# A convolution's banks, copies and order inside a two-block transformer kernel

## The chip, the cores and the metric

The kernel runs on one core of a Trainium2 chip. The metric is the device time of one execution in microseconds. TensorE multiplies matrices into PSUM banks, VectorE and ScalarE work on tiles of 128 partitions, GpSimd does some of the sums, and SyncE issues most of the DMAs; ScalarE and GpSimd can issue DMAs too. Every engine works through its own queue in order and waits on semaphores for the others.

## The reference, cut to what matters

The whole computes two small models one after the other on 512 tokens of width 1024. The change touches the first layer only:

```python
h = rms_norm(x, even_norm_g[j])
z = h @ even_w_in[j] + even_b_in[j]
za = gelu(z[..., :2 * A_WIDTH]); zb = z[..., 2 * A_WIDTH:]
ya = chunked_spatial_gating(za, ...)   # u * (w_s @ layer_norm(v) + b_s), u and v halves of za
yb = conformer_conv(zb, ...)           # silu(layer_norm(causal_dwconv(a * sigmoid(g), 31 taps)))
x = x + concatenate([ya, yb], -1) @ even_w_out[j]
```

Behind it come a feed-forward block, a layer of attention, a second feed-forward block, and two layers of the second model.

## The kernel before

Activations lie transposed: eight tiles of 128 features by 512 tokens. A product is taken in three fp32r matmuls (`mm3`, line 671): the high part of the weight with the high and the low part of the activation, and the low part of the weight with the high part. Weights stream in blocks through three staging buffers `stg`; ScalarE rounds a block to its high part `whi`, VectorE makes the low part `wlo`, and with that the staging buffer is free for the next load, which SyncE issues (`load`, `w_split`, `w_next`).

The program is written by a planner. Its `Clock` (line 318) holds a time for each engine and one for all DMAs together; `Engine` (line 373) charges each operation as it is traced, a DMA by its bytes at 180 GB/s. Work beside the dense products is written as generators, which `spawn` puts in a list with the time at which their last operation ended. `pump` runs every generator that is due by TensorE's planned time, and goes on until nothing moves; `need` pumps until a flag is set. The planner thus fixes an order in which the operations are traced. A scheduler then orders each engine's queue by its own estimate, except where `ORDERED` (line 677) names the weight segment: there the engines given by letters (V VectorE, A ScalarE, T TensorE) keep the traced order, in a region that `part()` opens at the head of a dense product.

The first layer, `even()`, runs in this order: the rms norm of the eight input tiles (`rms_part`; the squares are summed in `sqacc`, and `rms_rstd` takes statistics with eight TensorE instructions, a reciprocal on VectorE, and eight more to spread the result), then the dense products "zb" (64 weight steps of three matmuls, four steps to a block; five output tiles side by side, then three), "v0" (eight weight steps, each for four token tiles: 96 matmuls, over four banks at once), "u0" (96 matmuls) and "eout" (two halves of 96). The first matmul needs only the first input tile.

Of "zb" come the four gated tiles `hp[j]` (`zb_done`). The convolution of tile 0 is 31 operations on VectorE (`conv`). Tiles 1 to 3 are convolved on TensorE (`conv_pe`): 16 copies of 32 partitions shift `hp[j]` into four pages `R`, then 32 calls (64 instructions) of 32-column matmuls accumulate in one bank, and ScalarE takes it out. `conv_out` norms the four tiles: the centre, an approximate mean from two of them, is subtracted from all, then the moments are summed, and the SiLU ends it. `v_done` and `u_done` make the gating: VectorE norms the values, TensorE multiplies them with `ws` (16 instructions for each of four tiles), and the product with GELU(u) is the input of "eout".

The eight PSUM banks are in rings: three "D" for dense products, two "S" (scores of the attention later, and the gating products here), one each of "P", "O" and "G". "zb" takes its banks from "DS", "v0" from "DP", the convolution from "O", the norm's centre and spread from "P" and "O".

## Time and profile before

| | us |
|---|---|
| median of three timed runs (2489.49 to 2492.5) | 2492.15 |
| the profiled execution | 2487.64 |
| its span | 2485.9 |
| TensorE busy in the span | 2412.0 |
| VectorE / ScalarE / GpSimd busy | 1404.0 / 1078.8 / 346.6 |

A busy TensorE is not TensorE at its peak, since the ends of matmuls are modelled; how many matmuls a stretch holds, and at what granted clock, tells more. Idle time of an engine that nobody waits for costs nothing. Nearly all instructions are recorded by one helper, line 402, so that groups are told apart by their tiles.

### The profile page before, as it was taken

To read this page: it belongs to the slowest core of one execution; us is meant where nothing else is said; L and a number is where in the kernel's file an instruction comes from. 1 tells how busy PE (TensorE), PEld (TensorE's weight loads), DVE (VectorE), ACT (ScalarE), POOL (GpSimd) and SP (SyncE) were. 2 spreads that over 40 slices of the span, in tenths; PEclk is the share of its full clock that TensorE was granted. 3 is DMA by queue.
4 is the path that set the end of the run, shared out by engine and by line. 5 is a ranking of instruction groups with operands and counts; after the bars stand their busy time and mean duration, and the time that the engine had idled before them with its cause. 6 is when DMAs were issued, how large, how long until landed. Compare 5 with 4: busy or idle time off the path is not lost.

```text
span 2485.9 us, 31565 instructions
## 1 busy us (share of the span) xinstructions
PE 2412.0 (97%) x12311; PEld 1957.1 (79%) x12311; DVE 1404.0 (56%) x2477; ACT 1078.8 (43%) x1740; POOL 346.6 (14%) x447
## 2 busy tenths in 40 slices
PE   9999999999999999999999999999999989999997
PEld 7578888888766788888786688888897767888887
DVE  6666746743874773673665474343577455634345
ACT  4345424433874442443655543232346454423133
POOL 2011000010432100003221340000231023100003
PEclk9999999999999999999999999999999999999998
DMA  5322323222112222223131123323222101222321
GB/s 176 121 68 93 102 94 100 95 95 84 60 61 72 91 97 94 101 94 107 59 98 47 50 62 100 102 94 100 87 71 77 44 26 52 95 100 94 102 94 60
DMA packets 64646, 212.33 MB, mean 85 GB/s; under 512 B 8208, under 2 KB 10672, under 8 KB 64496
## 3 DMA queue, kind: packets, MB, share of 16 engines
q1 hardware_dynamic: 61200, 202.03, 24.8%
q0 software_dynamic: 2576, 6.82, 0.9%
q8 instruction: 97, 1.59, 0.3%
q10 hardware_dynamic: 720, 1.46, 0.2%
q14 instruction: 53, 0.43, 0.1%
HBM read 205.03 MB, written 2.10 MB: 83 GB/s over the span
## 4 chain that ended last, share of the span: by engine, by line
PE 57%; DVE 5%; ACT 2%; issue 1%; POOL 1%; ACTq 0%; DVEq 0%; POOLq 0%
PE bank L402 57%; DVE pt L402 3%; ACT pt L402 1%; DVE x L402 1%; DVE wlo L402 1%; ACT L402 1%; POOL x L402 1%; ACT whi L402 0%; POOL pt L402 0%; DVE pl L402 0%; ACT x L402 0%; POOL sqacc L402 0%; DVE stat L402 0%; ACT kend L402 0%; ACTq L2012 0%
## 5 line engine op out<-in xcount | busy, mean ns | idle before, releaser
L402 PE MATMUL bank<-pt,whi 128*128 128x512 f32 (+1 forms) x6012 | 1789.6, 380 | 20.2 <-ACT pt L402 9.3
L402 PEld LDWEIGHTS bank<-pt,whi 128*128 128x128 f32 x6012 | 1099.5, 189 | 232.5 <-ACT pt L402 13.5
L402 PE MATMUL bank<-pt,wlo 128*128 128x512 f32 (+1 forms) x3006 | 1131.9, 377 | 1.6 <-DVE wlo L402 1.6
L402 DVE TENSOR_TENSOR wlo<-stg,whi 128x1024 fp32r<-128x1024 f32 (+2 forms) x387 | 471.8, 1221 | 467.6 <-ACT whi L402 461.2
L402 ACT CAST whi<-stg 128x1024 fp32r<-128x1024 f32 (+2 forms) x387 | 394.1, 1020 | 676.9 <-PE bank L402 596.4
L402 PEld LDWEIGHTS bank<-pt,wlo 128*128 128x128 f32 x3006 | 568.3, 189 | 106.4 <-DVE wlo L402 2.9
L402 ACT CAST pt<-pt 128x512 fp32r<-128x512 f32 (+1 forms) x226 | 139.4, 620 | 243.5 <-DVE pt L402 208.2
L402 DVE TENSOR_TENSOR pt<-pt,pt 128x512 fp32r<-128x512 f32 (+2 forms) x235 | 165.1, 706 | 84.1 <-ACT pt L402 81.1
L402 DVE TENSOR_TENSOR x<-x,bank 128x256 f32<-128x256 f32 (+1 forms) x294 | 135.4, 497 | 132.9 <-PE bank L402 126.6
L402 PE MATMUL bank<-pt,pt 128*64 128x128 f32 (+17 forms) x1192 | 185.3, 387 | 13.2 <-ACT pt L402 6.6
L402 POOL TENSOR_TENSOR pt<-pt,pt 128x256 f32<-128x256 f32 (+1 forms) x90 | 98.1, 1098 | 458.6 <-ACT pt L402 234.9
L402 PEld LDWEIGHTS bank<-pt,pt 128*64 128x64 f32 (+4 forms) x1192 | 101.6, 152 | 76.1 <-issue 44.3
L402 DVE SCALAR_TENSOR_TENSOR pt<-up,cst,pt 128x512 f32<-128x512 f32 x176 | 131.9, 749 | 6.5 <-ACT pt L402 3.4
L402 POOL TENSOR_SCALAR pt<-pt,stat 128x512 f32<-128x512 f32 (+3 forms) x160 | 99.7, 643 | 236.4 <-DVE stat L402 211.0
L402 ACT COPY pt<-bank 128x512 f32<-128x512 f32 (+4 forms) x157 | 79.8, 508 | 116.9 <-PE bank L402 115.5
L402 PE MATMUL bank<-whi,pt 128*128 128x512 f32 (+2 forms) x448 | 124.1, 353 | 2.7 <-DVE pt L402 2.2
L402 PEld LDWEIGHTS bank<-misc,pt 128*128 128x128 f32 (+1 forms) x632 | 78.8, 160 | 50.7 <-issue 25.6
L402 PE MATMUL bank<-misc,pt 128*128 128x128 f32 (+2 forms) x632 | 103.0, 273 | 9.6 <-ACT pt L402 4.4
L402 DVE TENSOR_TENSOR up<-bank,rstd 128x512 f32<-128x512 f32 x88 | 60.6, 688 | 87.9 <-PE bank L402 83.5
L402 DVE CUSTOM_DVE_ANT_0 pt<-bank,mask 128x512 f32<-128x512 f32 (+3 forms) x160 | 75.7, 486 | 56.9 <-PE bank L402 56.2
L402 POOL TENSOR_TENSOR x<-x,pt 128x256 f32<-128x256 f32 x24 | 22.2, 961 | 591.0 <-ACT pt L402 591.0
L402 ACT ACTIVATE pt<-pt,stat 128x256 f32<-128x256 f32 (+3 forms) x160 | 89.3, 559 | 32.8 <-DVE stat L402 31.6
(147 smaller groups left out, 1379.4 us busy)
## 6 DMA issues: line engine op xcount, KB each, us to landing
stg<-in_w_up_dram SPq DMA_DIRECT2D x88, 512.0 KB, 3.2
stg<-in_w_mu_dram SPq DMA_DIRECT2D x64, 512.0 KB, 3.4
stg<-in_w_md_dram SPq DMA_DIRECT2D x44, 512.0 KB, 3.4
stg<-in_w_dn_dram SPq DMA_DIRECT2D x33, 512.0 KB, 3.2
stg<-in_w_qk_dram SPq DMA_DIRECT2D x16, 512.0 KB, 3.2
stg<-in_w_tb_dram SPq DMA_DIRECT2D x16, 512.0 KB, 3.5
stg<-in_w_zb_dram SPq DMA_DIRECT2D x16, 256.0 KB, 3.3
stg<-in_w_eout_dram SPq DMA_DIRECT2D x8, 512.0 KB, 3.3
```

The source lines that it names most:

```text
L402: r = fn(*a, **k)
```

## The change

Five edits in the first layer and in the planner. The planner's DMA charge takes the number of partitions from the tile instead of 128, and is at least 0.5 us. "zb" is added to the segments in traced order, for VectorE and TensorE; "v0", until now in traced order on TensorE, is so on VectorE too. Of the sixteen copies of a convolution tile, those for groups 0 and 2 are issued by SyncE and those for 1 and 3 by ScalarE. The convolution takes a bank from "O" or, where that is in use, from "S". The centre comes from tiles 1 and 0, and tiles 2 and 3 follow.

```diff
@@ Engine.__getattr__
-                nbytes = 4 * 128 * (out.free_size() if callable(out.free_size) else out.free_size)
-                self.clock.op("DMA", nbytes / 180e3, [out], [src])
+                nbytes = 4 * (out.free_size() if callable(out.free_size) else out.free_size)
+                nbytes *= out.partition_size() if callable(out.partition_size) else out.partition_size
+                self.clock.op("DMA", max(nbytes / 180e3, 0.5), [out], [src])
@@ tile_kernel
-    ORDERED = {"v0": "T", "u0": "T", "eout": "T", "qk": "VAT", "wo": "T", "tc0": "V", "tc1": "V", "na0": "V", "na1": "V",
+    ORDERED = {"zb": "VT", "v0": "VT", "u0": "T", "eout": "T", "qk": "VAT", "wo": "T", "tc0": "V", "tc1": "V", "na0": "V", "na1": "V",
                "tb0": "T", "tb1": "T", "out0a": "T", "out1a": "T"}
@@ conv_pe
                 for g in range(4):
                     for s in range(4):
-                        SY.dma_start(R[g][32 * s:32 * s + 32, :], hp[j][32 * g:32 * g + 32, 29 + s:541 + s])
+                        (SY, A)[g % 2].dma_start(R[g][32 * s:32 * s + 32, :], hp[j][32 * g:32 * g + 32, 29 + s:541 + s])
                 yield
-                b = yield from bank_task("O")
+                b = yield from bank_task("OS")
@@ conv_out
                 nm = Norm(C, 4, "eps6", "cln", slice(0, 512), new_shared(), "PO")
-                for j in (2, 3):
+                for j in (1, 0):
                     yield from until(("conv", j))
                     spawn(nm.first(j))
                 yield from until(("cln", "centre"))
-                for j in (1, 0):
+                for j in (2, 3):
                     yield from until(("conv", j))
                     V.tensor_tensor(C[j], C[j], nm.C, OP.add)
                     spawn(nm.late(j))
```

## Rows read from the trace of the kernel before

**Rows 1.** The page: busy time of each engine, and the chain that ended last.
```profile
PE 2412.0 (97%) x12311; PEld 1957.1 (79%) x12311; DVE 1404.0 (56%) x2477; ACT 1078.8 (43%) x1740; POOL 346.6 (14%) x447
...
PE 57%; DVE 5%; ACT 2%; issue 1%; POOL 1%; ACTq 0%; DVEq 0%; POOLq 0%
```

**Rows 2.** Busy time by stretch: busy us (instructions), clock, DMA share, GB/s.
```profile
core 0: us, PE busy (x) PEld busy (x) DVE busy (x) ACT busy (x) POOL busy (x), PEclk, DMA share, GB/s
...
8.20:24.19 15.99, 13.40 (x47) 10.65 (x48) 14.40 (x23) 12.29 (x23) 9.65 (x16) 0.81 0.87 303
24.19:58.60 34.41, 34.41 (x151) 28.22 (x149) 19.87 (x31) 9.97 (x15) 5.05 (x5) 0.99 0.30 88
58.60:74.60 16.00, 13.64 (x77) 4.34 (x76) 13.97 (x19) 3.33 (x4) 0.00 (x0) 1.00 0.65 193
74.60:103.50 28.90, 28.90 (x161) 19.99 (x161) 10.88 (x14) 7.69 (x9) 0.00 (x0) 1.00 0.39 126
103.50:147.20 43.70, 43.63 (x284) 31.32 (x282) 36.54 (x66) 23.68 (x34) 2.95 (x2) 0.96 0.19 61
147.20:155.00 7.80, 3.93 (x10) 2.93 (x11) 5.52 (x8) 5.49 (x8) 0.20 (x4) 0.78 0.00 0
```

**Rows 3.** Groups of TensorE's instructions from 8.2 to 24.15 us: count, busy, mean, idle before.
```profile
L402 PE MATMUL bank<-pt,whi 128*128 128x512 f32 x20 | 8.7, 515 | 3.2 <-ACT whi L402 2.4 <-ACT pt L402 0.8
L402 PE MATMUL bank<-pt,wlo 128*128 128x512 f32 x10 | 4.8, 477 | 0.0
```

**Rows 4.** Timeline of the start: start us, duration us, engine, operation, count.
```profile
8.26 2.50 PE L402 MATMUL bank<-pt,whi 128*128 128x512 f32 x5 [0.75 <-ACT pt L402]
...
18.15 0.69 DVE L402 TENSOR_TENSOR sqacc<-sqacc,pt 128x512 f32<-128x512 f32 x1
...
18.90 1.87 PE L402 MATMUL bank<-misc,sqacc 128*128 128x2 f32 x8
...
21.11 0.20 DVE L402 RECIPROCAL small<-small 128x8 f32<-128x8 f32 x1 [1.06 <-ACT small L402]
```

**Rows 5.** Timeline of SyncE's queue from 47 us.
```profile
47.49 11.09 SPq L402 DMA_DIRECT2D pt<-hp  x16
58.68 0.53 SPq L402 DMA_DIRECT2D stg<-in_w_v_dram  x1
59.31 0.40 SPq L402 DMA_DIRECT2D stg<-in_w_zb_dram  x1
```

**Rows 6.** Timeline of TensorE from 64 us.
```profile
64.93 0.73 PE L402 MATMUL bank<-pt,whi 128*128 128x512 f32 x2 [1.30 <-ACT whi L402]
...
74.62 0.50 PE L402 MATMUL bank<-whi,pt 128*128 128x512 f32 x1
...
86.43 6.89 PE L402 MATMUL bank<-pt,pt 128*32 128x512 f32 x64
```

**Rows 7.** Timeline of ScalarE from 47 us.
```profile
47.66 0.62 ACT L402 CAST whi<-stg 128x512 fp32r<-128x512 f32 x1 [0.90 <-ACT whi L402]
50.38 0.62 ACT L402 CAST whi<-stg 128x512 fp32r<-128x512 f32 x1 [2.10 <-PE bank L402]
51.58 0.73 ACT L402 ACTIVATE pt<-pt,cst 128x512 f32<-128x512 f32 x1 [0.57 <-DVE pt L402]
```

**Rows 8.** Timeline of the first microsecond: DMA issues on two queues.
```profile
0.74 0.41 ACTq L402 DMA_DIRECT2D x<-in_xT_dram  x1
...
0.75 0.39 SPq L402 DMA_DIRECT2D stg<-in_w_zb_dram  x1
```

**Rows 9.** Timeline of TensorE at 110 us.
```profile
109.79 6.89 PE L402 MATMUL bank<-pt,pt 128*32 128x512 f32 x64
116.60 1.09 PE L402 MATMUL bank<-ws,pt 128*64 128x128 f32 x16
```

**Rows 10.** Groups of VectorE's instructions from 103.5 to 151 us.
```profile
L402 DVE BATCH_NORM_STATS2 small<-pt 128x6 f32<-128x512 f32 x4 | 2.6, 669 | 0.0
```

**Rows 11.** Timeline of ScalarE and TensorE at 146 to 151 us.
```profile
146.09 1.28 ACT L402 ACT_TABLE_LOAD   x1
...
148.13 1.28 ACT L402 ACT_TABLE_LOAD   x1
...
150.80 0.52 PE L402 MATMUL bank<-pt,whi 128*128 128x512 f32 x1 [3.67 <-ACT pt L402]
```

## The prediction

> **What bounds the kernel now.** I read the page first: TensorE's instructions cover 97% of the span, and the chain that ended last is 57% TensorE [rows 1]. So a change pays only where TensorE stands or runs slowly, and all that it touches lies in the first 165 us. The table of busy time by stretch therefore came second [rows 2]. [...]
>
> [...]
>
> The end of the first projection, 58.6 to 74.6: TensorE does the 64 instructions of one convolution tile (6.9 us for such a block where nothing disturbs it) and the 12 matmuls of the last weight block (2.7 us), 9.6 us of work in 16.0 us: 6.4 us lost [rows 2, 6]. Why, the third view tells, SyncE's issues in order of time: sixteen copies of the first convolution tile hold its queue from 47.49 to 58.58, and only then leave a value weight block and the last block of "zb" (59.31) [rows 5].
>
> The end of the gating products, 147.1 to 154.7: TensorE waits 3.67 us for ScalarE, then does about 8 matmuls in 3.9 us at the lower clock, 2.0 us more than at 0.228 [rows 2, 11].
>
> **The parts of the change.** The work is the same; order, queues and banks change. I take the parts in order of time.
>
> *TensorE in program order in "zb".* The table puts T beside V there, and this costs at the start. The program traces eight rms parts, their statistics (8 instructions on `sqacc`) and only then the first matmul of "zb": a spawned task may run from the planner's last finish, which is by then the end of the `cst` load, so all eight rms parts are due at one instant, and `need` pumps until nothing more moves, the statistics included. Until now the scheduler put matmuls ahead: the first starts at 8.26, while VectorE finishes `sqacc` at 18.84 and the statistics start at 18.90 [rows 4]. In program order TensorE waits for `sqacc`, and VectorE makes the first low weight part only behind the reciprocal of 21.11. By 24.2 three matmuls are then done, not 30: 27 x 0.228 = 6.2 us later. [...] Bounds +5.0 to +7.2; I take +6.0, near the count. Nothing covers it: the stretch behind has no gap.
>
> *Half of the copies from ScalarE's queue.* Eight copies at 11.09/16 = 0.69 us hold SyncE for 5.5 us instead of 11.1. The weight load that left at 59.31 then leaves about 5.6 us earlier relative to TensorE, and lands while TensorE is at the convolution tile, for which the copies are there by 47.49 + 5.5 + 2 = 55. So up to 6.4 us come back; bounds 0 (below) to -6.4. I take all of it, as the 5.6 us and the convolution's 6.9 us together cover the gap. What is late next is ScalarE. Its eight issues, from 47.49 to 53.0, stand ahead of the rounding of a weight block that now starts at 47.66 [rows 7]. TensorE needs this block two blocks of 12 matmuls later, at 52.9; it would have it at 53.6, its low part at 54.3: 0 to 1.4 us, I take 0.7. Behind the issues wait also the next rounding (50.38) and the sigmoid (51.58), which delays the second tile only; its convolution has a whole projection to wait in. The same queue is passed by the second and third tiles' issues, where the weight blocks last 5.4 us and are two ahead: nothing.
>
> That two engines issue side by side in the time of one, the trace shows only at its first microsecond: ScalarE's issue of 0.41 and SyncE's of 0.39 overlap in full, and a lone SyncE issue of the same size takes 0.40 [rows 5, 8]. [...]
>
> *Score banks for the convolution, and the DMA cost in the planner.* A 32-partition copy was charged as a 128-partition one, so the planner traced the second tile's convolution behind 51 value matmuls and the third inside "u0" (at 109.79). Now both come inside the value products. Moved work, 6.9 us each: zero by itself. The banks are two that "zb" leaves idle: zero. But the third tile's 6.9 us stood between the value products and the first gating product (116.60), and hid VectorE's layer norm of the values [rows 9]. That cover goes; VectorE has 36.5 us of work in 43.7 us there [rows 2].
>
> *VectorE in program order* in "zb" and "v0": it is idle for 18 of the 28.9 us from 74.6 [rows 2]; its order costs nothing beside the start. Bounds 0 to +1.
>
> *Centre from tiles 0 and 1.* Both are there before the value products end, but the centre needs the "P" bank, which "v0" holds to its end; so it comes just behind "v0" instead of behind the third tile. The convolution's SiLU leaves the end of "u0". There ScalarE now swaps its table twice, 1.28 us each, between the last gating tile's GELU and its rounding [rows 11]. Without both swaps 3.67 - 2.56 = 1.1 us of the wait stays, with one 2.4: I take 1.8 saved. Bounds 0 and 5.7 (wait and lower clock both gone).
>
> Beyond the block the planner's small DMA charges (at least 0.5 us) alter the traced order a little: plus or minus 2 us.
>
> Sum: +6.0 - 6.4 + 0.7 - 1.8 = -1.5 us. Against the profiled execution of 2487.6 this is 2486.1. The three timed runs lie higher (2489.5 to 2492.5), and the sum is set on their median: 2492.15 - 1.5 = **2490.7 us**. About 0.2% (5 us) is what a measurement of this kernel can tell from no change.
>
> **The rivals.** *The gating products come too early (slower).* The planner charges VectorE by output columns: a BATCH_NORM_STATS2 with six output columns at 0.07 + 6 x 0.00104 = 0.08 us, where the trace has 0.669 [rows 10], and no table load of 1.28 us at all. Four of the first and three of the second are 6.2 us that it doesn't see; the matmuls are charged 0.213 for 0.228, which takes back about 1. In program order TensorE then stands at the first gating product, which was covered by the convolution tile: 5 us, and the 1.8 aren't saved. -1.5 + 1.8 + 5 = +5.3: 2497.5. It decides once fewer than 54 matmuls (12.2 us, the time from the end of "v0" to the last norm product) stand ahead of the product. For it: the cover goes. Against: the convolution norm's own products fill part of it.
>
> *The issues don't overlap.* Sixteen copies take 11.1 us from two queues too. The weight load leaves as late as before, and ScalarE's rounding of 47.66 ends at 59.2, so TensorE stands ahead of that block instead of behind it: nothing of the 6.4 us comes back, and the +0.7 is inside. +6.0 - 1.8 = +4.2: 2496.4.
>
> *The start costs nothing (faster).* If the scheduler's order on TensorE still puts matmuls ahead of the statistics, -1.5 - 6.0 = -7.5: 2484.6. For it: only that the table entry might act on less than I read. Against: in "v0", in program order already, the convolution block stands as a whole behind 51 matmuls [rows 6], as it is traced.
>
> **How the numbers follow.** Forecast 0.47, gating products early 0.20, no overlap 0.10, start free 0.17, other orders further on 0.06. Forecast alone: from its bounds 2485 to 2496. The range takes in the start-free case and the gating case: 2484 to 2498. Faster by over 0.2% (under 2487.2): 0.16 of the start-free case, 0.12 of the forecast (tail at its far bound), 0.03 of the rest: 0.31. Slower (over 2497.1): 0.13 of the gating case, 0.05 of no overlap, 0.03 of the forecast, 0.03 of the rest: 0.24. Within: 0.45.
>
> **What would show it.** In the profile after: the first "zb" matmul behind the statistics, near 20 us, and block ends 6 us later up to the end of "zb"; SyncE's and ScalarE's bursts of eight copies of 5.5 us each; the third tile's convolution inside the value products; no table load between the last GELU and its rounding, and a wait of 1 to 2.4 us there. The prediction is wrong if the first matmul stays at 8 us, if the bursts last 11 us, or if TensorE stands some 5 us at the first gating product.

## The result and the profile after

| | before | after |
|---|---|---|
| median, same chip (5 runs each) | 2489.49 us (2487.18 to 2492.5) | 2509.38 us (2505.33 to 2517.03) |
| ratio | 1 | 1.0087 (95% interval 1.0072 to 1.0101) |
| profiled execution, its span | 2487.64, 2485.9 us | 2508.27, 2506.5 us |

The change costs 20 us. The prediction, 2490.7 with a range to 2498, was wrong in size and on the wrong side of "no change".

The page of after has TensorE busy for 5.6 us more than in [rows 1], and the chain that ended last is TensorE's for 57% as before. That doesn't say where 20 us went; marks along the first layer do. I counted the weight matmuls in TensorE's timeline (a few records are missing, so each mark is good to about 0.3 us):

| from, to | before | after | difference |
|---|---|---|---|
| start of the span to half of "zb" (matmul 97) | 39.5 | 47.2 | +7.7 |
| to the end of "zb" (193) | 35.1 | 30.1 | -5.0 |
| to the end of the values "v0" (289) | 29.0 | 35.9 | |
| to the first weight load of the feed-forward block | 65.9 | 69.6 | |
| the last two together | 94.9 | 105.5 | +10.6 |
| the rest of the span | 2316.4 | 2323.7 | +7.3 |

The last two stretches of the first layer are taken together, since the third convolution tile (6.9 us) moves from one to the other. The sum is 13.3 us in the layer that the change touches and 7.3 behind it. The stretches of after, cut at these marks, answer to [rows 2]: busy time in us (instructions) of TensorE, its weight loads, VectorE, ScalarE and GpSimd, then TensorE's granted clock, DMA share and GB/s.

```profile
8.20:24.19 15.99, 5.28 (x20) 4.47 (x21) 12.83 (x18) 10.97 (x19) 9.57 (x17) 1.00 0.72 252
...
66.20:77.30 11.10, 11.10 (x83) 5.46 (x83) 10.78 (x16) 3.42 (x5) 0.00 (x0) 1.00 0.56 163
...
113.20:157.00 43.80, 38.06 (x214) 31.63 (x214) 33.93 (x62) 25.19 (x34) 2.76 (x2) 0.84 0.14 46
157.00:164.00 7.00, 1.73 (x10) 0.73 (x6) 3.50 (x6) 6.94 (x10) 0.20 (x4) 0.82 0.05 19
```

TensorE's busy time at the start fell from 13.40 to 5.28 us. The end of "zb" is clean: 11.10 us of 11.10. From 113.2 on, 5.74 + 5.27 = 11.0 us are idle (before: 0.07 + 3.87), and the granted clock is 0.84, where it was 0.96.

The start, timelines of TensorE and VectorE, and of GpSimd:

```profile
18.82 1.87 PE L402 MATMUL bank<-misc,sqacc 128*128 128x2 f32 x8 [11.32 <-DVE sqacc L402]
20.55 1.20 PE L402 MATMUL bank<-pt,whi 128*128 128x512 f32 x2
...
28.47 0.50 PE L402 MATMUL bank<-pt,wlo 128*128 128x512 f32 x1 [1.30 <-DVE wlo L402]
```

```profile
21.14 8.47 DVE L402 TENSOR_TENSOR wlo<-stg,whi 128x512 fp32r<-128x512 f32 x4
```

```profile
21.79 6.07 POOL L402 TENSOR_TENSOR pt<-misc,cst 128x512 f32<-128x512 f32 x6
```

TensorE's first weight matmul stands behind the statistics, as forecast. What I hadn't seen: four low weight parts, 0.69 us each where VectorE makes them alone, take 8.47 us beside GpSimd's six products, which build the convolution's weights.

The copies of the first convolution tile, on SyncE's and ScalarE's queues, and TensorE's timeline of the tile:

```profile
55.80 5.32 SPq L402 DMA_DIRECT2D pt<-hp  x8
...
61.80 0.46 SPq L402 DMA_DIRECT2D stg<-in_w_zb_dram  x1
```

```profile
55.81 5.63 ACTq L402 DMA_DIRECT2D pt<-hp  x8
...
62.12 0.60 ACT L402 CAST whi<-stg 128x512 fp32r<-128x512 f32 x1
```

```profile
65.11 0.50 PE L402 MATMUL bank<-pt,wlo 128*128 128x512 f32 x1 [0.98 <-DVE wlo L402]
66.23 6.89 PE L402 MATMUL bank<-pt,pt 128*32 128x512 f32 x64
80.80 6.89 PE L402 MATMUL bank<-pt,pt 128*32 128x512 f32 x64
98.72 6.89 PE L402 MATMUL bank<-pt,pt 128*32 128x512 f32 x64
```

Two engines issue sixteen copies in 5.6 us, where one took 11.09 [rows 5]. All three tiles run in one piece, and the third (98.72) now lies inside the value products; before it stood at 109.79, behind them [rows 9].

The gating stretch, timelines of VectorE and of TensorE:

```profile
129.35 1.21 DVE L402 TENSOR_TENSOR wlo<-stg,whi 128x1024 fp32r<-128x1024 f32 x1
```

```profile
130.62 0.80 PE L402 MATMUL bank<-pt,wlo 128*128 128x512 f32 x1 [5.74 <-DVE wlo L402]
131.35 3.30 PE L402 MATMUL bank<-ws,pt 128*64 128x128 f32 x32
...
159.12 0.50 PE L402 MATMUL bank<-pt,whi 128*128 128x512 f32 x1 [1.84 <-ACT pt L402]
...
163.79 1.52 PE L402 MATMUL bank<-pt,whi 128*128 128x512 f32 x2 [3.05 <-ACT pt L402]
```

TensorE stands 5.74 us for a low weight part whose rounded half ScalarE had at 122.9 (its cast starts at 121.86 and takes 1.04); VectorE makes it only at 129.35, behind the values' layer norm. Behind that wait the granted clock is 0.68 from 130.6 to 140 us, 0.53 to 144.6 and 1.00 from there to 157; and at the end TensorE waits for ScalarE in three places (1.84, 0.39 and 3.05 us; before in two, 3.67 and 0.28).

VectorE has more ahead of this low part than in before. There the low part was the first of two at 115.70, and the convolution norm's centre was added at 121.54; in after the centre is added at 115.29. Here are VectorE's lines of before, then the one of after:

```profile
115.70 2.35 DVE L402 TENSOR_TENSOR wlo<-stg,whi 128x1024 fp32r<-128x1024 f32 x2
...
121.54 1.29 DVE L402 TENSOR_TENSOR pt<-pt,bank 128x512 f32<-128x512 f32 x2 [0.30 <-ACT pt L402]
```

```profile
115.29 1.25 DVE L402 TENSOR_TENSOR pt<-pt,bank 128x512 f32<-128x512 f32 x2
```

Counted from the end of the last value product (103.7 in before, 113.3 in after), the low part is ready after 13.2 us in before and after 17.3 in after. Ahead of it now stand six instructions of the convolution's norm, 4.0 us, that before has behind it; the other differences nearly cancel. TensorE came for the low part after 11.6 us. So of the wait of 5.74, some 4 us are this work of VectorE's and some 1.7 the rest; that is an estimate from the two traces, and no run takes the six instructions out.

### The profile page after: what moved, and what is told of

It reads as the page before. It is cut to its first block, busy times and chain, and to the rows that moved or that the text cites. A ratio compares the mean times of both kernels' runs of the same rounds, so it can differ in the third digit from the quotient of the medians.

```text
span 2506.5 us, 31564 instructions
## 1 busy us (share of the span) xinstructions
PE 2417.6 (96%) x12311; PEld 1964.9 (78%) x12311; DVE 1408.9 (56%) x2477; ACT 1083.8 (43%) x1744; POOL 344.8 (14%) x447
## 4 chain that ended last, share of the span: by engine, by line
PE 57%; DVE 5%; ACT 2%; issue 1%; POOL 1%; ACTq 0%; DVEq 0%; POOLq 0%
PE bank L402 57%; DVE pt L402 3%; ACT pt L402 1%; DVE x L402 1%; DVE wlo L402 1%; ACT L402 1%; POOL x L402 1%; ACT whi L402 0%; POOL pt L402 0%; DVE pl L402 0%; ACT x L402 0%; POOL sqacc L402 0%; ACT kend L402 0%; ACTq L2013 0%; DVE stat L402 0%
## 5 line engine op out<-in xcount | busy, mean ns | idle before, releaser
L402 ACT ACTIVATE pt<-pt,stat 128x256 f32<-128x256 f32 (+3 forms) x160 | 89.4, 559 | 33.0 <-DVE stat L402 31.9
```

The source lines that it names most:

```text
L402: r = fn(*a, **k)
```

## Experiments: each edit alone, or left out

Every kernel ran in three rounds or more beside the kernel before on the same chip. The table at the end of the last experiment has the marks of all of them.

**The changed kernel with the table of orders of before.** TensorE and VectorE in "zb", and VectorE in "v0", go back to the scheduler.

```diff
-    ORDERED = {"zb": "VT", "v0": "VT", "u0": "T", "eout": "T", "qk": "VAT", "wo": "T", "tc0": "V", "tc1": "V", "na0": "V", "na1": "V",
+    ORDERED = {"v0": "T", "u0": "T", "eout": "T", "qk": "VAT", "wo": "T", "tc0": "V", "tc1": "V", "na0": "V", "na1": "V",
```

> The changed kernel with the table of traced orders as it was before (no "zb", "v0" on TensorE alone). Theory A (three separate losses: the start by the order on TensorE, the gating by VectorE being crowded behind the value products, the later stages by the planner's DMA charge): only the start comes back, the first matmul of "zb" at about 8 us, first layer 7 us shorter, total 2502 us. Rival B (the order on VectorE is what crowds the gating, too): the gating's 10 us come back as well, 2492 us.

Measured 2509.49 us, ratio 1.0081 (1.0058 to 1.0104). The start is back (first matmul at 9.0, half of "zb" at 39.9), but nothing came of it: "zb" needs 37.6 us for its second half instead of 30.1, and the wait of 5.7 us in the gating stretch is there as in after. So VectorE's order in "zb" and "v0" isn't its cause, and the program order that costs at the start pays at the end of "zb".

**The changed kernel with the DMA charge of before.**

```diff
-                nbytes = 4 * (out.free_size() if callable(out.free_size) else out.free_size)
-                nbytes *= out.partition_size() if callable(out.partition_size) else out.partition_size
-                self.clock.op("DMA", max(nbytes / 180e3, 0.5), [out], [src])
+                nbytes = 4 * 128 * (out.free_size() if callable(out.free_size) else out.free_size)
+                self.clock.op("DMA", nbytes / 180e3, [out], [src])
```

> The changed kernel with the planner's DMA charge as it was before. Theory A: the convolution tiles are traced late again, the gating stretch and the later stages return to their times before, the start's 7 us stay and the copies' gain of about 5 stays: 2489 to 2494 us; the later stages (from the first feed-forward's weights to the end) as long as before. Rival C (the centre from tiles 0 and 1 makes the gating's loss): the gating keeps its 10 us, 2500 us.

Measured 2503.73 us, ratio 1.0060 (1.0037 to 1.0083). The third tile is back behind the values, and values and gating together take 94.0 us, as before (94.9) and not 105.5. That much of the total isn't seen, because its start is worse than that of after: half of "zb" comes at 54.2, after a wait of 6.19 us for a low weight part.

**The kernel before with the new charge alone.**

> The kernel before with the planner's new DMA charge alone. Theory A: start unchanged; gating +5 to +10 us, since the third convolution tile leaves it; the stages behind the first layer +7 us as in the changed kernel: 2500 to 2507 us. Rival D (the later 7 us come from whatever changes the first layer's end, not from the charges in the second model): later stages within 2 us of before, 2494 to 2500.

Measured 2503.0 us, ratio 1.0055 (1.0033 to 1.0076): one edit of a planner's cost, on a kernel with the old queues, banks, centre and order, costs 13.6 us. TensorE's timeline:

```profile
95.70 6.89 PE L402 MATMUL bank<-pt,pt 128*32 128x512 f32 x64
...
127.61 0.80 PE L402 MATMUL bank<-pt,wlo 128*128 128x512 f32 x1 [5.74 <-DVE wlo L402]
128.34 3.15 PE L402 MATMUL bank<-ws,pt 128*64 128x128 f32 x32
```

The third tile lies in the values, and the wait is the very 5.74 us of after.

**The kernel before with the new order alone.**

> The kernel before with "zb" in traced order on VectorE and TensorE and "v0" on VectorE too, nothing else. Theory A: the first matmul of "zb" waits for the statistics (about 20.5 us), the first layer is 7 us longer, the rest as before: 2496 us. Rival B: also the gating gets longer, 2500 us or more.

Measured 2503.29 us, ratio 1.0055 (1.0033 to 1.0078). Half of "zb" at 46.2 (+6.7); then the second half takes 37.8 us, since sixteen copies on one queue hold the last weight block (they leave from 54.79 to 65.92, its load at 66.59) and TensorE, in program order, stands 5.33 us for it. Values and gating take 95.6 us: no loss there. The order's price is the start; without the second queue it gets nothing back.

## Experiments: what the 6.4 us at the end of "zb" were

Before's own timeline of TensorE, in lines not shown so far, contradicts my reading of that stretch:

```profile
60.07 3.56 PE L402 MATMUL bank<-pt,pt 128*32 128x512 f32 x28 [0.39 <-issue]
...
67.29 0.50 PE L402 MATMUL bank<-pt,wlo 128*128 128x512 f32 x1 [0.67 <-DVE wlo L402]
...
69.31 1.01 PE L402 MATMUL bank<-pt,pt 128*32 128x492 f32 x2
70.25 0.49 PE L402 MATMUL bank<-pt,whi 128*128 128x512 f32 x1
70.68 1.01 PE L402 MATMUL bank<-pt,pt 128*32 128x492 f32 x2
71.62 0.49 PE L402 MATMUL bank<-pt,wlo 128*128 128x512 f32 x1
```

One weight matmul and two convolution matmuls take 71.62 - 70.25 = 1.37 us; at their undisturbed prices, 34.41/151 = 0.228 us [rows 2] and 6.89/64, they are 0.228 + 2 x 6.89/64 = 0.44. Each excursion of TensorE from 128-column to 32-column matmuls and back thus costs 0.93 us here. The scheduler made five of them between 58.6 and 74.6, where one is needed: 4 x 0.93 = 3.7 us. The idle time that the timeline shows is 0.39 + 1.30 + 0.67 = 2.4 us [rows 6 has the 1.30]. Together 6.1 of the 6.4. I had put all of it on the late weight block.

The other profiles bear the price out. In the changed kernel with the orders of before the tile is in ten pieces, and the second half of "zb", with no wait in it, takes 37.6 us:

```profile
60.48 1.04 PE L402 MATMUL bank<-pt,pt 128*32 128x512 f32 x2
61.46 0.49 PE L402 MATMUL bank<-pt,wlo 128*128 128x512 f32 x1
61.88 1.05 PE L402 MATMUL bank<-pt,pt 128*32 128x512 f32 x2
```

The kernel with the charge alone has seven pieces, no wait, and 35.0 us. After has one piece, and 30.1 us of which 0.98 are a wait. The same 160 matmuls thus take 29.1 us in one piece, and each further piece adds 0.94 us in the first of these kernels and 0.98 in the second. The granted clock is 1.00 in all three.

**The kernel before with two queues and the score banks.**

```diff
-                        SY.dma_start(R[g][32 * s:32 * s + 32, :], hp[j][32 * g:32 * g + 32, 29 + s:541 + s])
+                        (SY, A)[g % 2].dma_start(R[g][32 * s:32 * s + 32, :], hp[j][32 * g:32 * g + 32, 29 + s:541 + s])
...
-                b = yield from bank_task("O")
+                b = yield from bank_task("OS")
```

> The kernel before with half of the copies issued by ScalarE and with the score banks allowed, and nothing else. Theory P (the prediction's): the 6.4 us lost from 58.6 to 74.6 are time that TensorE stands behind a late weight block; with the copies on two queues they come back, and the first layer ends 5 to 6 us earlier: about 2484. Theory I (interruptions): of those 6.4 us only 1.30 + 0.67 + 0.39 = 2.4 are idle in the timeline of before; the other 4.0 are the price of switching between dense matmuls and 32-column matmuls (a pair of these with one dense matmul takes 1.37 to 1.40 us, where 0.23 + 2 x 0.108 = 0.44 would do). Copies that come earlier only start the switching earlier: in the charge-alone kernel against the one with charge, queues, banks and centre, zb ends at 74.3 against 77.5. So here zb ends 0 to 3 us later than before, the total is 2489 to 2493 where the rest of the span keeps its length, and 3 to 5 more where later stages lose as they did in the other four kernels.

Measured 2485.37 us against 2488.06, ratio 0.9992 (0.9978 to 1.0006). The total can't tell the two theories apart, the marks can: the second half of "zb" takes 32.6 us instead of 35.1. That is the idle 2.4 us and no more; the tile is still in five pieces, and no wait is left: 32.6 - 29.1 = 3.5 us for four further pieces. I had expected that more pieces would eat the gain, and they didn't.

**The kernel before with two queues, and TensorE in program order from the second pass of "zb" on.** The start is left to the scheduler.

```diff
+            if i == late:
+                region.append(tc.manual_schedule(engines={nc.tensor.engine}))
+                region[0].__enter__()
...
-            dense_t(SEQ_ZB, XH, XL, xf, zb_done, "DS")
+            dense_t(SEQ_ZB, XH, XL, xf, zb_done, "DS", late=40)
```

> The kernel before with half of the copies on ScalarE's queue, and with TensorE in program order in zb only from its second pass on (weight steps 40 to 63), so that the start is left to the scheduler. The banks, the charge and the centre stay as before. Theory I: first matmul near 8.3; the convolution tile stands undisturbed (6.9 us) ahead of the last weight block; zb ends near 68.5 instead of 74.6 (2.4 of idle and 4.0 of switching gone, 0 to 1 given back to ScalarE's late rounding), the third tile stays inside u0, so the gating stretch keeps its length: first layer 5 to 6 us shorter, 2484. Theory P gives the same here; what would speak against both is zb ending after 72. Later stages: by theory T (below, next kernels) they lose or gain some us by their new time alone, so 2482 to 2490 in all.

Measured 2484.24 us against 2488.06, ratio 0.9978 (0.9966 to 0.9991): faster than both kernels in these executions, by a margin that the repeat below leaves open. The second half of "zb" takes 31.1 us, 4.0 less than before. Of the 2.1 us missing to 6.1, small waits ahead of the tile are 1.0 and the tile itself, 7.32 us instead of 6.89, is 0.4; the granted clock reads 1.00 there, so why it is longer stays open, as does the rest:

```profile
58.69 0.50 PE L402 MATMUL bank<-pt,wlo 128*128 128x512 f32 x1 [0.46 <-DMA pt<-hp]
59.12 7.32 PE L402 MATMUL bank<-pt,pt 128*32 128x512 f32 x64
```

So the 6.4 us were two losses. Two queues take one, program order the other, and after has both; its -5.0 is their sum, -2.4 - 3.7, less the late rounding's 0.98.

## Experiments: the stages behind

After lost 7.3 us behind the first layer, and most variants so far lost some there. In after itself the new charge lets 29 TensorE instructions between 1223.8 and 1229.2 us stand at other places than in before, and one on VectorE and one on ScalarE. In the kernel with the order alone, no engine's order of instructions differs from before once the first layer is over. Two stretches, from the first weight load of "tc" to that of "nb" and from that of "out0a" to that of "out0b", in the columns of the first table, of before:

```profile
1192.74:1217.19 24.45, 23.25 (x197) 21.09 (x195) 15.88 (x27) 12.85 (x24) 3.60 (x2) 1.00 0.25 76
...
1302.65:1364.01 61.36, 57.53 (x415) 41.54 (x413) 35.20 (x103) 34.53 (x70) 8.29 (x11) 1.00 0.13 44
```

of after:

```profile
1207.35:1233.11 25.76, 24.68 (x197) 22.44 (x196) 15.74 (x27) 12.88 (x24) 3.58 (x2) 0.93 0.27 82
...
1318.50:1382.92 64.42, 60.60 (x415) 43.87 (x413) 35.17 (x103) 34.51 (x70) 8.29 (x11) 0.95 0.14 42
```

and of the kernel with the order alone:

```profile
1200.85:1226.64 25.79, 24.68 (x197) 22.32 (x196) 15.83 (x27) 12.83 (x24) 3.60 (x2) 0.93 0.21 71
...
1312.13:1377.92 65.79, 61.94 (x415) 45.09 (x413) 35.20 (x103) 34.52 (x70) 8.31 (x11) 0.92 0.13 41
```

The same number of instructions and hardly other idle time (24.45 - 23.25 = 1.20, 25.76 - 24.68 = 1.08, 1.11): what differs is the granted clock. The waits ahead of the first of these stretches are the same too, here before and then after:

```profile
1200.63 0.30 PE L402 MATMUL bank<-pt,cw 128*64 128x62 f32 x2 [0.81 <-PE bank L402]
```

```profile
1215.23 0.30 PE L402 MATMUL bank<-pt,cw 128*64 128x62 f32 x2 [0.81 <-PE bank L402]
```

**The kernel before with a pure delay.** 58 repeated matmuls in the first up product, 13.2 us, and in a second kernel 22, 5.0 us.

```diff
+            if m == 1 and c == 0:
+                for _ in range(pad):
+                    nc.tensor.matmul(bank[mh][:, cs], wh, xh[k][:, cs], start=True, stop=True, skip_group_check=True)
             mm3(bank[mh][:, cs], wh, wl, xh[k][:, cs], xl[k][:, cs], c == 0, c + 1 == total[mh])
```

> The kernel before with 58 more matmuls (the first matmul of the second output tile of the first up product, repeated into its own bank, which the real product then overwrites): 58 x 0.228 = 13.2 us of fed TensorE, the delay that the changed kernel has at this place. All else keeps its order on every engine but for five neighbouring instructions at the padding itself. Nothing of the computation is left out. Theory T (time): the later stages of all variants are longer by 3 to 6 us because the same waits fall at another time, and the granted clock falls at some of them and not at others (behind wo, at tc1, at out0a). Then a pure delay does it too: the total is 13.2 plus 2 to 7, 2505 to 2510, with granted clocks below 1.00 in tc1 or out0a, where before has 1.00. Theory N (the new order or the new charge makes the later stages longer): they keep their length here, and the total is 2489.4 + 13.2 = 2502.6, within 1 us.

> As the kernel with 58 more matmuls, with 22: 5.0 us of delay. Theory N: 2494.4, within 1 us, all later stages as long as before. Theory T: 2494.4 plus something between -2 and +6, and the stages at which the clock falls are not those of the kernel with 58: the excess doesn't grow with the delay.

Measured 2511.2 us, ratio 1.0071 (1.0045 to 1.0098), and 2499.08 us, ratio 1.0041 (1.0026 to 1.0057), against 2488.06. The stretches of the kernel with 58:

```profile
1208.59:1234.44 25.85, 24.75 (x197) 22.45 (x196) 15.83 (x27) 12.84 (x24) 3.58 (x2) 0.93 0.24 69
...
1319.90:1384.33 64.43, 60.60 (x415) 43.85 (x413) 35.19 (x103) 34.50 (x70) 8.29 (x11) 0.95 0.12 42
```

A delay alone gives the clocks of after, 0.93 and 0.95, and the same lengths within 0.1 us. In its profiled execution the delay of 13.2 us costs 25.6 us, and that of 5.0 costs 18.2: the excess, some 12 to 13 us, doesn't grow with the delay. In the times the effect is less clear. The ten executions of the kernel with 22 matmuls lie from 2495.1 us, at a mean granted clock of 0.986, to 2507.12 at 0.981, and the interval of the kernel with 58 takes in the 13.2 us without excess (ratio 1.0053), while that of the kernel with 22 leaves out 5.0 us (1.0020). So I hold the 7.3 us for no work of the change's: behind the same wait of 0.81 us the clock is 1.00 in before and 0.93 in after.

The profiles of the kernels without repeated matmuls say the same more plainly. Behind the first layer nine of them have every engine's order of before, and that rest of the span takes from 2314.3 to 2323.6 us (before 2316.4); nine have the order of after, and it takes from 2316.7 to 2327.3 (after 2323.7). The late-order kernel's two profiles, of one program, are 5.1 us apart there (2321.7 and 2316.6). So 7.3 us is what two profiles can differ by with no change at all. What decides it, and how much of it the medians hold, stays open.

## Experiments: the gating stretch

**The changed kernel with the centre from tiles 2 and 3.**

```diff
-                for j in (1, 0):
+                for j in (2, 3):
                     yield from until(("conv", j))
                     spawn(nm.first(j))
...
-                for j in (2, 3):
+                for j in (1, 0):
```

> The changed kernel with the centre taken from tiles 2 and 3 again. Theory M (cover): the gating stretch is 10.6 us longer (from the end of the value products to the first up weight load, 69.6 us, against 65.9 less the 6.9 of the third convolution tile) because the new charge traces that tile into the value products, so that nothing covers VectorE's layer norm; the centre has no part in it. Then the wait of 5.7 us for the low weight part stays, and the total is 2507 to 2511. Theory C (centre): the earlier centre crowds VectorE with the convolution norm, and mixes SiLUs with GELUs on ScalarE; then the wait shrinks to under 3 us, two table loads go, and the total is 2502 to 2505.

Measured 2507.17 us, ratio 1.0070 (1.0050 to 1.0091). The wait of 5.74 us stays; values and gating take 103.8 us instead of 105.5. The centre isn't the cause. That it costs here rather than saves isn't shown: two profiles of one program differ as much (94.6 and 96.3 us for the late-order kernel).

**The changed kernel with VectorE in program order in "u0" too.**

> The changed kernel with VectorE in program order in u0 too, so that the low weight part stands about 13 instructions earlier in VectorE's queue, ahead of a part of the values' layer norm. Theory M1 (the low part stands too late): TensorE gets the block some 5 us earlier, the wait of 5.74 us goes, and with it part of the lower clock behind it: 2499 to 2504. Theory M2 (VectorE is full, so any order leaves a hole): the wait moves to the first gating product, which then waits for the layer norm, and the total stays at 2507 to 2511.

Measured 2518.91 us, ratio 1.0106 (1.0081 to 1.0132): slower by 9.5 us than after, against both theories. Its start has the wait of 6.39 us for a low weight part, as the kernel with the old charge had; and in the gating stretch two low parts are late, by 2.33 and 5.62 us. So this traced order isn't the cure. A clock that charges VectorE too little may be why; no run changes those charges.

**The changed kernel with the third tile held back by hand.** Its copies go as early as in after, its matmuls wait for the norm's centre, and so stand 15 weight matmuls behind the end of the values. The charge stays new.

```diff
+                if j == 3:
+                    yield from until(("cln", "centre"))
                 b = yield from bank_task("OS")
```

> The changed kernel, with the third convolution tile's matmuls (not its copies) held by hand until the norm's centre is there, so that its 64 instructions stand in u0 again, 15 dense matmuls behind the end of the value products. Everything else, the new charge too, is as in the changed kernel. Theory M (cover): the wait of 5.74 us for the low weight part goes or falls under 1 us, and with it the stretch at the lower clock behind it; from the end of the value products to the first up weight load it takes 66 us with the tile, as before, instead of 69.6 without it; the total is 2497 to 2501. Theory M2 (VectorE has too much to do there, whatever TensorE does): the hole only moves, the stretch takes 69.6 + 6.9 = 76.5, and the total stays at 2507 to 2511.

Measured 2497.67 us against 2488.46, ratio 1.0032 (1.0019 to 1.0046): 9.2 us over its own before, where after was 19.9 over its own. TensorE's timeline, then VectorE's at the low part:

```profile
114.97 6.89 PE L402 MATMUL bank<-pt,pt 128*32 128x512 f32 x64
130.08 3.63 PE L402 MATMUL bank<-misc,pt 128*128 128x2 f32 x32
133.63 2.98 PE L402 MATMUL bank<-ws,pt 128*64 128x128 f32 x32
```

```profile
127.91 2.35 DVE L402 TENSOR_TENSOR wlo<-stg,whi 128x1024 fp32r<-128x1024 f32 x2
```

The wait is gone, values and gating take 94.2 us, and their granted clock is 0.96 (0.90 in after). The same work at another place, 6.9 us of cover, is worth 11 us there; this profile's start has a wait of 6.08 us for a low part, so that the total shows less of it. VectorE is no faster than in after: the low part is ready 17.7 us behind the last value product (17.3 in after), with the same six instructions of the convolution's norm ahead of it, and TensorE comes for it at 129.85, just behind. This shows that the place of the tile is the cause, and that its cover alone takes the wait away, with the centre and VectorE's load as they are in after. Whether VectorE making that low part earlier would do it too, with the tile inside the values, isn't shown: the one other order tried in "u0" was worse.

## Experiments: both losses undone, and what stays

**The changed kernel with program order from the second pass of "zb" on** (as above, for TensorE only), **and the same with the old charge.**

> The changed kernel with TensorE in program order in zb from its second pass on only (weight steps 40 to 63), and VectorE in zb left to the scheduler. First matmul near 9 instead of 20.6, and zb ends at 68 to 70 instead of 77.3, as in the late-order kernel of the second experiment. The gating stretch keeps its 5.7 us wait (theory M). So the first layer ends about 8 us earlier than in the changed kernel: 2500 to 2503, and the loss against before that is left, 11 to 14 us, is the price of the charge. If the order of the first pass were harmless, the total would stay near 2509.

> The same with the DMA charge of before as well: queues, banks, centre and VectorE's order in v0 are as in the changed kernel. Theory M: the third convolution tile stands in u0 again and the gating stretch is as long as before or 1 to 2 us shorter (centre); zb ends near 68.5. So the total is 2481 to 2485, 4 to 8 us under before. If the centre or VectorE's order were to blame for the gating stretch, it stays some 10 us too long, and the total is 2491 to 2495.

Measured 2497.06 us against 2489.49, ratio 1.0024 (1.0006 to 1.0042), and 2490.08 us, ratio 0.9999 (0.9987 to 1.0011). The first is better than expected, 12.3 us under after. Its profile has 7.3 us of that in "zb" and gives 2.4 back in the gating; the other 7.0 lie behind the first layer, in the scatter of the section on the stages behind. So "zb" is worth about 7 here. The second misses by 5 us: values and gating are the shortest of all (93.5 us), but a rounding behind ScalarE's copies comes 1.87 us late, and the convolution tile after that wait takes 8.94 us:

```profile
62.22 0.73 PE L402 MATMUL bank<-pt,whi 128*128 128x512 f32 x2 [1.87 <-ACT whi L402]
63.38 8.94 PE L402 MATMUL bank<-pt,pt 128*32 128x512 f32 x64
```

The granted clock from 62.2 to 72.4 is 0.83. Behind the wait of 1.87 us the tile thus takes 8.94 - 6.89 = 2.05 us more. With the start and the charge both undone, then, nothing is left of the 19.9 us that the change cost: 2490.08 is 0.6 over before.

**The late-order kernel with the new centre.**

> The late-order kernel of the second experiment (two queues, TensorE in program order in the second pass of zb, the charge of before) with the centre from tiles 1 and 0. The traces with the old charge take 64.4 and 65.2 us from the end of the value products to the first up weight load with this centre, and 65.8 to 66.7 with the old one: 1 to 2 us of gain, so 2482 to 2484, against 2484.2 of the late-order kernel. If the later centre was harmless and the difference came from the score banks or VectorE's order, it stays at 2484 to 2486.

Measured 2491.69 us against 2488.46, ratio 1.0002 (0.9990 to 1.0014): no gain from the centre, and 7 us over the late-order kernel. Values and gating take 95.6 us, against 94.6 in that kernel.

**GpSimd's products later.** Called behind the first output tile of "zb", they ran at 22.07 all the same, since nothing on GpSimd made them wait; so this kernel tells nothing of its question (2512.75 us, ratio 1.0088, 1.0071 to 1.0106).

> The changed kernel, with GpSimd's six products for the convolution weights not at 22 us but behind the first output tile of zb (some 35 us). Theory G (GpSimd holds VectorE up): in the changed kernel four low weight parts took 8.47 us beside these six products, where one takes 0.69 alone, and in two other kernels with the same order three took 7.9 and 8.2 us and TensorE stood 6.2 and 6.4 us. Without the overlap the low parts behind the reciprocal take 0.7 us each, TensorE's wait of 1.30 us at 28 us goes, and the total is 1 to 5 us under the changed kernel: 2504 to 2508. Rival: the low parts are slow there for another cause (the weight loads that land then); they still take 1.5 us or more each, and the total is 2508 to 2511.

With a copy of that tile ahead of them on GpSimd they do wait:

```diff
+                    if m == 0:
+                        with tc.issue_after(G.tensor_copy(small[:, 78:79], p[:, 0:1]).ins):
+                            build()
```

> The changed kernel, with GpSimd's six products for the convolution weights behind a copy, on GpSimd itself, of the first output tile of zb; so they can't start before about 36 us (in the kernel with the products called later without such a copy they still ran at 22.07). Theory G (one of VectorE's and GpSimd's instructions holds the other up): the low parts behind the reciprocal at 21 to 22 us take 0.7 us each, as alone, TensorE's wait for them at 28 us (1.30 in the changed kernel, 6.0 to 6.4 in four others of this order) goes, and near 36 us it is some other VectorE instruction that is held, where TensorE is blocks ahead. Total 2505 to 2508. Rival (weight loads or the lower clock slow them): the low parts still take 1.5 us or more each without GpSimd beside them, and the total is 2508 to 2513.

VectorE's first low weight parts in the first of the two kernels, with GpSimd beside them, and then in the second, without:

```profile
22.16 7.72 DVE L402 TENSOR_TENSOR wlo<-stg,whi 128x512 fp32r<-128x512 f32 x3
```

```profile
21.27 1.84 DVE L402 TENSOR_TENSOR wlo<-stg,whi 128x512 fp32r<-128x512 f32 x3
```

That settles who slows them. The total is 2511.32 us against 2489.16 (1.0085, 1.0066 to 1.0104) and misses the 2505 to 2508: the products now run from 51.11 on, beside the first convolution tile on VectorE, and TensorE waits there for four low parts (0.66, 0.22, 1.08 and 0.35 us).

**The late-order kernel with GpSimd's queue in place of ScalarE's, and the late-order kernel again.**

```diff
-                        (SY, A)[g % 2].dma_start(R[g][32 * s:32 * s + 32, :], hp[j][32 * g:32 * g + 32, 29 + s:541 + s])
+                        (SY, G)[g % 2].dma_start(R[g][32 * s:32 * s + 32, :], hp[j][32 * g:32 * g + 32, 29 + s:541 + s])
```

> The late-order kernel (old charge, old centre, TensorE in program order in the second pass of zb) with the second half of the copies from GpSimd's queue instead of ScalarE's. If ScalarE's issues are what delays the rounding ahead of the convolution tile (waits of 0.3 to 1.9 us for the rounded part, after which the tile takes 7.3 to 8.9 us at the lower clock instead of 6.9), these waits go, the tile takes 6.9, and the median is 1 to 3 us under the late-order kernel's. Rival: GpSimd issues more slowly (0.52 us each for its early loads, against 0.69 for a copy on SyncE, speaks against it), or holds VectorE up while it does, and the median is the same or up to 3 us more.

> The late-order kernel of the second experiment again, beside the kernel before in more rounds, since its sister with the other centre came out 7 us above it, more than the traces of the two explain (4.6 us at the end of the first layer, 3 of them lost ahead of the second pass, where both have the same order). If its gain of 0.22% is real, the ratio is 0.9975 to 0.999 again; if it was the luck of which waits met the lower clock, the interval takes in 1.

Measured 2486.63 us against 2489.16, ratio 0.9988 (0.9977 to 1.0000), and 2484.77 us, ratio 0.9991 (0.9976 to 1.0005). GpSimd's queue doesn't help: the tile takes 7.22 us, after a wait of 1.14 us for a rounding that no longer stands behind copies; the granted clock around it reads 1.00, so the lower clock of the expectation isn't seen there. The late-order kernel's median is 4 us under before's in both of its runs (22 executions); but of the two intervals one excludes 1 and one doesn't, so a gain of 0.1 to 0.2% is likely and not settled.

The marks of all profiles but the two with repeated matmuls (us; a: half of "zb"; b: its second half; c: values and gating to the first load of the feed-forward block):

| kernel | a | b | c |
|---|---|---|---|
| before | 39.5 | 35.1 | 94.9 |
| after | 47.2 | 30.1 | 105.5 |
| after, order of before | 39.9 | 37.6 | 108.3 |
| after, charge of before | 54.2 | 31.9 | 94.0 |
| before, charge alone | 39.3 | 35.0 | 105.2 |
| before, order alone | 46.2 | 37.8 | 95.6 |
| before, queues and banks | 40.7 | 32.6 | 96.0 |
| late order (two profiles) | 37.4, 40.5 | 31.1, 31.3 | 94.6, 96.3 |
| late order, new centre | 40.2 | 31.3 | 95.6 |
| late order, GpSimd's queue | 40.4 | 31.1 | 96.4 |
| after, old centre | 45.9 | 30.1 | 103.8 |
| after, VectorE ordered in "u0" | 52.9 | 29.9 | 113.0 |
| after, late order | 40.7 | 29.3 | 107.9 |
| after, late order and old charge | 40.6 | 33.8 | 93.5 |
| after, third tile held | 52.5 | 29.9 | 94.2 |
| after, GpSimd's products called later | 53.0 | 30.1 | 107.8 |
| after, GpSimd's products at 51 | 46.8 | 32.6 | 105.6 |

Column c has two groups with nothing between: 93.5 to 96.4 where the third tile stands behind the values, 103.8 and more where it stands inside. Column a has three: 37 to 41 without program order in the first pass, 46 to 47 and 52 to 54 with it. Two profiles of one program differ by 3 us in a, which bounds what one profile can tell.

## Why the prediction was wrong, step by step

**Start, +6.0: right in kind, short in size.** 7.7 measured. The matmuls wait for the statistics as worked out, 27 of them at the 0.228 us of [rows 2] (34.41 us for 151): the 6.2 us of the count. The lower bound of +5.0 counts on VectorE to end `sqacc` up to 1.2 us earlier; it ends at 18.76, 0.08 us before the 18.84 of before. The upper bound of +7.2 holds 1 us for a lower clock after the time without work, an estimate of the author's that no run shows; what after shows behind its 11.32 us of wait is a low-part matmul of 0.79 us at 21.84, where one of before takes 0.63 at 21.20, and from 24.95 on 0.39 us in after for 0.40 in before; the granted clock of after's stretch from 8.20 to 24.19 reads 1.00. Most of the rest of the 7.7 is the wait of 1.30 us from the collision of VectorE and GpSimd, which in four of the seven other profiles with this order cost TensorE 6.0 to 6.4 us in one wait. The profile of before had GpSimd's six products at 22.03, of 7.21 us, in the stretch of [rows 4]; I had added nothing for the low parts behind the reciprocal, 0.69 us each where VectorE makes them alone, without looking who else works there.

**Copies and the gap, -6.4 + 0.7: the sum nearly right, its reason wrong.** -5.0 measured. Only 2.4 of the 6.4 us were waits; 3.7 were excursions, which the copies don't touch and the program order of "zb" takes away. I had counted that order as a pure cost. The stretch had told it: in [rows 2] TensorE is busy 13.64 of 16.0 us, so no more than 2.4 can be waiting. The late rounding cost 0.98 us where I took 0.7.

**Banks and charge at zero: the step that failed.** "Moved work, 6.9 us each: zero by itself" was followed by the right warning, that the cover of VectorE's layer norm goes, and I left it to a rival with a chance of 0.20. In all eight profiles with the tile inside the values the stretch is 9 to 18 us longer than the 94.9 of before; no other edit is needed for it. What the runs showed in place of "zero by itself" is 10.6 us in after and 10.3 with the charge alone, and a stretch 11.3 us shorter again with the tile held behind the values. The rival had the place and the engine right: VectorE is busy for 10.00 us of 120 to 130 in after. It expected the hole at the first gating product; it came one step earlier, at a low weight part that VectorE makes behind the layer norm. The argument set against it, that the convolution norm's products fill part of the hole, went the other way: they come behind the hole, at 134.57, and the norm's six VectorE instructions come ahead of the low part and make the hole longer. The rival's 5 us were the wait of 5.74 alone. The other half, 10.6 - 5.7 = 4.9 us, are 1.4 more of waits at the end (5.27 idle for 3.87) and 3.5 by which TensorE's busy time is longer for the same matmuls, with a granted clock of 0.90 over the two stretches for 0.96. I had no term for a lower clock behind this hole.

**Centre, -1.8: not seen.** In after the SiLUs fall between the last GELUs, with five table loads from 150.03 to 161.12 instead of the two of [rows 11], and TensorE waits 1.84 + 0.39 + 3.05 us for what was 3.67 + 0.28. With the old charge c is 93.5 to 95.6 with the new centre and 94.6 to 96.4 with the old: a gain of about 1 us, inside the scatter.

**Issues don't overlap: false.** The trace of after has 5.32 us for eight copies on one queue and 5.63 for eight on the other, at the same time, where sixteen on one queue took 11.09 [rows 5].

**Start free of charge: false**, by the first matmul at 20.55.

**Downstream, plus or minus 2: too narrow.** +7.3 in the profile, with the same clocks in a kernel that is only delayed. Other kernels with after's order of instructions there take 2316.7 us and more, so the order doesn't explain it; the profiles scatter by 9 to 11 us at this place, which no bound of mine allowed for.

With the terms as measured the sum is 7.7 - 5.0 + 10.6 + 7.3 = 20.6 us, the difference of the two spans. Of the medians' 19.9 us, the late order alone takes 12.3 off and the held tile alone 10.7, each set against its own before. That is more together than there is to take off; the scatter behind the first layer may be why, which isn't shown.

## What to carry to other kernels

Work that moves is not free because it is the same work: ask what it covered, and price what comes behind the hole too: here 3.5 us more of busy time came with a wait of 5.74 (granted clock 0.90 for 0.96), and 2.05 more with one of 1.87 (0.83), while behind one of 1.14 the clock read 1.00. Read a stretch's loss as idle time first and slow instructions second, as a gap of 6.4 us with 2.4 idle is mostly something else than waiting. A planner's price list is part of the program: a charge that is more correct for one copy moved a tile away from where it covered VectorE, and cost 10 us. Whether better prices for VectorE would have kept it there, no run tests.

## What the runs showed of the hardware

*VectorE and GpSimd hold each other up.* In thirteen of the twenty profiles GpSimd's six products take 6.1 us and one or more VectorE instructions beside them stand for as long: 7.28 us for a product with `ws` that takes 1.17 alone. In six others GpSimd takes 7.2 to 7.6 us and no VectorE instruction stands that long (1.53 us for a low part); the late-order kernel did it either way in its two profiles. With GpSimd's products moved away three low parts took 1.84 us, beside them 7.72. So a VectorE instruction may stand for all six products; what the two engines share is not shown.

*Leaving the 128-column matmuls for 32-column ones and coming back costs 0.9 to 1.0 us* in the rows above: 0.93 in before, 0.94 and 0.98 for each further piece in the two kernels with ten and seven. That is the price of the whole excursion; no run takes it apart.

*GpSimd issues these copies faster than SyncE or ScalarE*: eight in 3.97 us, 0.50 each, in the one kernel that does so, against 0.63 to 0.75 for the first tile's on the other two queues. Between 48 and 64 us of that kernel's profile they also land later, 4.7 us in the median from the issue, where SyncE's took 3.0.

*The granted clock differs between executions of one program.* The kernel with 22 repeated matmuls took 2495 us at a mean clock of 0.986 and 2507 at 0.981 on the same chip.
